# Convolution taps spread over the products of a stage, and a retention cut into 16 pieces between dense products

## The chip, the cores and the metric

One Trainium2 chip, of which the program uses one core. The metric is the device time of one execution in microseconds; the time of a kernel is the median of its runs. The engines of the core are named as in the profile: PE (TensorE matmuls) and PEld (its weight loads), DVE (VectorE), ACT (ScalarE), POOL (GpSimd), SP (SyncE, which issues the transfers).

## The reference

Two blocks follow one another, each with two layers, on a sequence of 1024 tokens of width 1024 in float32. A layer of the first block mixes three branches (a gated convolution of width 256, windowed attention, gated linear attention) and also carries a context of 256 tokens. A layer of the second block mixes spatial gating, a pooling over several scales and a retention, and has a feed-forward part behind it. The two parts that the change touches:

```python
def _conv_branch(p, conv_w, conv_b, ln_w, ln_b):        # first block
    u = p['a_val'] * jax.nn.sigmoid(p['a_glu'])
    u = lax.conv_general_dilated(u, conv_w[:, None, :], window_strides=(1,), padding=((15, 15),), ...,
                                 feature_group_count=256) + conv_b      # 31 taps, channel by channel
    u = (u - mean(u)) * lax.rsqrt(var(u) + NORM_EPS) * ln_w + ln_b
    return jax.nn.silu(u) * jax.nn.silu(p['a_gate'])

def retention(q, k, v, g, norm_g):                      # second block: 8 heads of 64, 8 chunks of 128
    ...
    scores = jnp.einsum('bnthd,bnshd->bnhts', qc, kc) * d_intra
    y_intra = jnp.einsum('bnhts,bnshe->bnthe', scores, vc)
    kv = jnp.einsum('bnshd,bnshe->nbhde', kc * k_dec[:, :, None], vc)
    _, s_prev = lax.scan(lambda state, kv_n: (state * chunk_dec + kv_n, state), zeros, kv)
    y_cross = jnp.einsum('bnthd,nbhde->bnthe', qc * q_dec[:, :, None], s_prev)
    y = group_norm(y_intra + y_cross)                   # mean and variance over each head's 64
    return jax.nn.silu(g) * (y * norm_g)
```

## The kernel before

**Dense products.** Every dense product is three matmuls of split operands (`mm3`, L211 to L213: hi × hi, hi × lo or lo × hi). ACT makes the high half of a weight (`whi`, L205), and its low half (`wlo`) is a subtraction on POOL (L190) or DVE (L192); in the projections of the first block four of six go to POOL (`LP_L1`). `gemm_fm` has the weights stationary: one product is 24 matmuls of 512 columns (or 256 for the context). `gemm_tm` has the tokens stationary: one token block is 24 matmuls of the weight's width (288 columns in `tm2`, 384 in `tm1`, 512 in `v` and `za`). After the evacuation of each product or token block `tick()` is called: it takes one mark off `self.ticks`, and when none is left it advances a generator, `self.side`, by one step. What a step emits lies behind that product in the program.

**Order on the engines.** A scheduler places the instructions; each engine runs its own queue in order. A high priority moves instructions ahead in it, and `in_order()` keeps PE's instructions of a block as they are written.

**The convolution (first block, both layers).** `conv_taps` (L469 on) makes 4 sums in layer 0, each of a first product and 30 taps on DVE (L482, L484): `ca20` and `ca21` for the context, 256 wide, and `ca00` and `ca01` for the sequence, 1024 wide. In layer 1 there are 60 taps, on 1024. Within a sum every tap reads the one before. All taps are emitted at once, before `qk`, with a high priority (offset -1500). `qk` makes the queries and keys, rotates them on DVE (`qt`, `qra`, `qrb`, `qa`, L821 to L827), splits them (`qlo`) and stores them over SP. Behind it `gla_proj` runs `tm2` (ten token blocks, with the copies `lr` and the gates `ggt`), the weights W12 and W11, and `tm1`. `conv_out` (the mean and variance over channels by matmuls with the constants `om` and `ones`, the normalisation and the gate) is the side generator of `gla_proj`, behind `CT` = 15 or 13 marks.

**The retention (second block, both layers).** `rotate` writes rotated queries and keys to memory. `gemm_tm` "v" makes the values of the eight blocks. Then `retention` emits all eight blocks in one go. Each has the scores of two groups of heads (L1234, 64 rows of the array each, first one half of the rows, then the other; the score times the decay is `ra`, L1236), the transposed keys (L1241, `kd` L1243), the score times the values (L1248), the state times the queries (L1256, one half of the rows after the other, `ry` L1257 and L1258), the new state (L1266, between halves of the columns; `rst` L1272 and L1273) and the norm of the result on DVE, POOL and ACT (`rmu`, `rv`, `rsq`, `rss`, with a power on POOL, L179). Keys and queries of each block come by transfer (L1227) in two buffers. The projection and the sums of the pooling (`pooling_in`, `pooling`) and the gating's projection `za` (`spatial_in`) follow.

## Time and profile before

| | |
|---|---|
| runs | 3634.89, 3642.01 and 3643.11 us, median 3642.01 |
| profiled execution | 3637.38 us, its span 3635.6 us |
| mean granted clock of PE | 0.975 |
| busy: PE, PEld | 3439.9 us (95%), 2757.1 us (76%) |
| busy: DVE, ACT, POOL | 2448.4 us (67%), 1209.4 us (33%), 848.1 us (23%) |

The profile is of one execution. The views below are: the page's account of the chain of work that ended last, by engine; stretches of time (start and end, length, then for PE, PEld, DVE, ACT and POOL the busy microseconds and in brackets the instructions, the clock granted to PE as a share of full speed, the share of the transfer engines and GB/s); the waits of an engine (the waiting line, the operation that released it, total, times, longest); pieces of the chain and instructions in time (start, duration, engine, line, operation, in square brackets the idle time ahead and what ended it); and groups of instructions (count, busy time, mean ns, idle time ahead). Names of tiles have their buffer numbers left out.

### The profile page before, as it was taken

Reading aid. Unit: us, or ns where it says so; the run is one execution under the profiler, and the core shown is the slowest. Engines: PE = TensorE matmul, PEld = TensorE weight load, DVE = VectorE, ACT = ScalarE, POOL = GpSimd, SP = SyncE. Lnnn points to the kernel's source line nnn. Section 1 sums busy time; section 2 is a strip of 40 time slices with the busy share of each in tenths; the row PEclk is TensorE's granted clock in tenths of the full one; section 3 lists DMA queues with packets and bytes.
Section 4 is the critical chain, followed back from the end, with each engine's and each line's share of the span. In section 5 each row is a group of like instructions: output and inputs, shape, how many; then the busy total and the mean of one; then the engine's idle time right before and its main releaser. Section 6 shows DMA issues by size and latency. Waiting matters only on the chain.

```text
span 3635.6 us, 47069 instructions
## 1 busy us (share of the span) xinstructions
PE 3439.9 (95%) x17414; PEld 2757.1 (76%) x17414; DVE 2448.4 (67%) x3786; ACT 1209.4 (33%) x2189; POOL 848.1 (23%) x700
## 2 busy tenths in 40 slices
PE   7959999998899999999999998999999989999898
PEld 4858766786776678887878776887887778877786
DVE  5963568569365867364599999446363589999545
ACT  4114236341251642213343334223112333334322
POOL 4331332112323222040133222001041132232100
PEclk9979999999899999999999999999999999999999
DMA  5221355533224234314422222434322522221532
GB/s 198 74 76 63 109 163 163 179 117 82 67 71 123 77 118 126 107 39 136 134 79 78 85 70 82 161 96 151 93 68 88 176 75 76 81 76 59 185 99 90
DMA packets 245973, 380.71 MB, mean 105 GB/s; under 512 B 29104, under 2 KB 103792, under 8 KB 245232
## 3 DMA queue, kind: packets, MB, share of 16 engines
q1 hardware_dynamic: 245744, 377.71, 33.4%
q8 instruction: 137, 2.24, 0.3%
q14 instruction: 92, 0.75, 0.1%
HBM read 280.35 MB, written 97.26 MB: 104 GB/s over the span
## 4 chain that ended last, share of the span: by engine, by line
PE 56%; DVE 15%; issue 5%; DMA 2%; ACT 2%; POOL 2%; SPq 0%; DVEq 0%; POOLq 0%; ACTq 0%
PE mm L213 10%; PE mm L211 10%; PE mm L212 10%; PE ax L211 3%; PE ax L213 3%; PE ax L212 3%; PE sc L211 3%; PE sc L213 3%; PE sc L212 3%; DVE wlo L192 2%; DVE cv L1427 2%; DVE ca L484 1%; DVE fth L331 1%; PE ax L1248 1%; PE sc L1234 1%
## 5 line engine op out<-in xcount | busy, mean ns | idle before, releaser
L211 PE MATMUL mm<-hi,whi 128*128 128x512 f32 (+1 forms) x1780 | 688.8, 387 | 22.5 <-ACT whi L205 12.4
L213 PE MATMUL mm<-hi,wlo 128*128 128x512 f32 (+1 forms) x1780 | 687.8, 386 | 5.1 <-DVE wlo L192 5.1
L212 PE MATMUL mm<-lo,whi 128*128 128x512 f32 (+1 forms) x1780 | 684.4, 385 | 1.2 <-DVE lo L1612 1.1
L205 ACT CAST whi<-wraw 128x512 fp32r<-128x512 f32 (+3 forms) x412 | 231.9, 583 | 583.9 <-PE mm L212 260.5
L192 DVE TENSOR_TENSOR wlo<-wraw,whi 128x512 fp32r<-128x512 f32 (+2 forms) x320 | 231.6, 738 | 279.0 <-ACT whi L205 277.6
L211 PEld LDWEIGHTS mm<-hi,whi 128*128 128x128 f32 x1780 | 336.6, 189 | 94.4 <-ACT whi L205 13.2
L213 PEld LDWEIGHTS mm<-hi,wlo 128*128 128x128 f32 x1780 | 336.0, 189 | 75.7 <-DVE wlo L192 8.2
L212 PEld LDWEIGHTS mm<-lo,whi 128*128 128x128 f32 x1780 | 336.4, 189 | 72.2 <-DVE lo L1612 3.1
L190 POOL TENSOR_TENSOR wlo<-wraw,whi 128x512 fp32r<-128x512 f32 (+3 forms) x92 | 138.3, 1510 | 796.4 <-ACT whi L205 768.6
L211 PE MATMUL sc<-hi,whi 128*128 128x512 f32 x732 | 288.4, 394 | 18.2 <-ACT whi L205 10.5
L213 PE MATMUL sc<-hi,wlo 128*128 128x512 f32 x732 | 288.5, 394 | 2.0 <-DVE wlo L192 1.9
L212 PE MATMUL sc<-lo,whi 128*128 128x512 f32 x732 | 287.6, 393 | 2.0 <-DVE lo L1612 1.9
L211 PE MATMUL mm<-whi,hi 128*128 128x512 f32 (+2 forms) x704 | 260.5, 370 | 20.9 <-ACT whi L205 15.7
L212 PE MATMUL mm<-wlo,hi 128*128 128x512 f32 (+2 forms) x704 | 256.3, 364 | 11.9 <-POOL wlo L190 10.8
L213 PE MATMUL mm<-whi,lo 128*128 128x512 f32 (+2 forms) x704 | 256.8, 365 | 0.0
L484 DVE SCALAR_TENSOR_TENSOR ca<-u,wh,ca 128x1024 f32<-128x1024 f32 (+1 forms) x180 | 184.6, 1079 | 0.6
L213 PE MATMUL ax<-hi,wlo 128*128 128x512 f32 x456 | 180.1, 395 | 2.4 <-DVE wlo L192 2.4
L211 PE MATMUL ax<-hi,whi 128*128 128x512 f32 x456 | 180.1, 395 | 1.8 <-DVE xn L1343 1.4
L212 PE MATMUL ax<-lo,whi 128*128 128x512 f32 x456 | 179.2, 393 | 0.0
L211 PEld LDWEIGHTS sc<-hi,whi 128*128 128x128 f32 x732 | 138.7, 189 | 49.3 <-ACT whi L205 11.2
L192 DVE TENSOR_TENSOR wlo<-wr,whi 128x512 fp32r<-128x512 f32 x200 | 175.3, 887 | 0.0
L211 PEld LDWEIGHTS mm<-whi,hi 128*128 128x128 f32 x704 | 134.5, 191 | 40.5 <-ACT whi L205 15.9
(376 smaller groups left out, 6737.5 us busy)
## 6 DMA issues: line engine op xcount, KB each, us to landing
wr<-in_w_up SPq DMA_DIRECT2D x80, 512.0 KB, 3.5
wraw<-in_w_fm SPq DMA_DIRECT2D x108, 256.0 KB, 3.1
wm<-in_w_mod SPq DMA_DIRECT2D x96, 256.0 KB, 3.7
wraw<-in_w_down SPq DMA_DIRECT2D x96, 256.0 KB, 2.7
hid_d<-fth SPq DMA_DIRECT2D x44, 512.0 KB, 2.6
wraw<-hid_d SPq DMA_DIRECT2D x88, 256.0 KB, 2.9
wraw<-in_w_out SPq DMA_DIRECT2D x80, 256.0 KB, 3.4
yl<-y_d SPq DMA_DIRECT2D x64, 256.0 KB, 3.1
```

The costliest lines, as they stand in the source:

```text
L190: nc.gpsimd.tensor_sub(out, x, f(hi))
L192: nc.vector.tensor_sub(out, x, f(hi))
L205: nc.scalar.copy(hi[:, c], r)
L211: nc.tensor.matmul(ps, sh, mh, start=start, stop=False)
L212: nc.tensor.matmul(ps, sh, ml, start=False, stop=False)
L213: nc.tensor.matmul(ps, sl, mh, start=False, stop=stop)
L331: nc.vector.scalar_tensor_tensor(out, tanh_tmp, 1.0, x, op0=ALU.add, op1=ALU.mult)
L484: nc.vector.scalar_tensor_tensor(a, u[:, j:j + n], wh[:, c, j:j + 1], a, op0=ALU.mult, op1=ALU.add)
L1234: nc.tensor.matmul(ps[:, m * 128:m * 128 + 128], k[r, m, :], q[r, m, :], start=True, stop=True)
L1248: nc.tensor.matmul(pi[:, hv], A[h % 2][:, h // 2, :], V[:, j, hv], start=True, stop=True)
L1427: nc.vector.scalar_tensor_tensor(t[:, o:], x[:, 0:S - o], wc(2 - o), t[:, o:], op0=ALU.mult, op1=ALU.add)
```

## The change

`conv_taps` becomes a generator. It yields after every tap of 1024 columns and after every fourth of 256, works one sum after the other (`ca20`, `ca21`, `ca00`, `ca01`), and has no priority. Each tap gets a dependency on the last `mm3` matmul emitted (`not_before`), which only the scheduler sees: it becomes no wait on the chip. The generator is advanced by the ticks of `qk` (one step a tick, two in the products of `ev_a`) and of `gla_proj` (two steps, and three from W12 on); `conv_out` is chained behind it.

`retention` becomes a generator of 16 pieces, two for a block. It is created ahead of "v" and advanced by its ticks (after two idle ones, `RT`), by those of `pooling_in` and by those of `za`; what is left runs behind `spatial_in`. Score matmuls and state matmuls now alternate between the two halves of the rows, in a fixed order. The keys and queries of the next block are loaded behind the first piece of a block; the values for the new state stand before the score times the values; `pooling` stands before `spatial_in`.

```diff
+    def not_before(self, ins):
+        self.tc.add_manual_dep(
+            ins.ins, self.mark.ins.name,
+            mybir.DependencyInfo(mybir.DependencyClass.NoSync, mybir.DependencyReason.SCHED_ONLY), reason="pace")
@@ mm3
-        nc.tensor.matmul(ps, sl, mh, start=False, stop=stop)
+        self.mark = nc.tensor.matmul(ps, sl, mh, start=False, stop=stop)
@@ tick
-                next(self.side, None)
+                for _ in range(self.pace):
+                    next(self.side, None)
@@ layer1
-                self.conv_taps(l, conv, cp)
+                taps = self.conv_taps(l, conv, cp)
+                self.ticks, self.side, self.pace = [], taps, 1
                 self.qk(l, W, both, al, rng)
...
-                    self.ticks = [None] * CT[l]
-                    self.side = self.conv_out(l, conv, cl)
+                    self.side, self.pace = chain(taps, self.conv_out(l, conv, cl)), 2
@@ conv_taps
-                with self.tc.high_priority(offset=-1500):
-                    nc.vector.tensor_scalar(a, u[:, 0:n], wh[:, c, 0:1], self.col("conv_b", 2 * l + c), op0=ALU.mult, op1=ALU.add)
-                    for j in range(1, 31):
-                        nc.vector.scalar_tensor_tensor(a, u[:, j:j + n], wh[:, c, j:j + 1], a, op0=ALU.mult, op1=ALU.add)
+                self.not_before(nc.vector.tensor_scalar(a, u[:, 0:n], ...))
+                for j in range(1, 31):
+                    self.not_before(nc.vector.scalar_tensor_tensor(a, u[:, j:j + n], wh[:, c, j:j + 1], a, ...))
+                    if j % (S // n) == 0:
+                        yield
@@ layer2
-            self.gemm_tm("v", I["w_tm_v"][l], 512, toks(), ev_v)
-                self.retention(l, V, rp, r1)
+                self.ticks = [None] * RT
+                self.side = self.retention(l, V, rp, r1)
+                self.gemm_tm("v", I["w_tm_v"][l], 512, toks(), ev_v)
                     xb = self.pooling_in(l, W, lat, mp)
+                    self.pooling(l, xb, mp)
                     z = self.spatial_in(l, toks, sp)
-                    self.pooling(l, xb, mp)
+                    run(self.side)
@@ retention
+            with self.in_order():
+                for m in range(4):
+                    for g, r in halves:
+                        nc.tensor.matmul(ps[g][:, m * 128:m * 128 + 128], k[r, m, :], q[r, m, :], start=True, stop=True)
...
+                nxt = load(j + 1)
+            yield
...
+                with self.in_order():
+                    for m in range(4):
+                        for g, r in halves:
+                            nc.tensor.matmul(pc[g][:, m, :], q[r, m, :], st[r, m, :], start=True, stop=True)
...
+            yield
```

On DVE in layer 0, where `qk` ends and `tm2` begins, the kernel before has the constants of `conv_out` (`lwh`, `om`) and the first copies of `tm2` behind the taps, of which only a few are left:

```order
L484 SCALAR_TENSOR_TENSOR ca_1000<-u_600,wh,ca_1000 128x1024
L484 SCALAR_TENSOR_TENSOR ca_968<-u_609,wh,ca_968 128x256
L484 SCALAR_TENSOR_TENSOR ca_1032<-u_603,wh,ca_1032 128x1024
L484 SCALAR_TENSOR_TENSOR ca_936<-u_606,wh,ca_936 128x256
L492 TENSOR_SCALAR lwh<-cols 128x1
L493 TENSOR_SCALAR lwh<-cols 128x1
L492 TENSOR_SCALAR lwh<-cols 128x1
L493 TENSOR_SCALAR lwh<-cols 128x1
L495 MEMSET om 128x128
L484 SCALAR_TENSOR_TENSOR ca_968<-u_609,wh,ca_968 128x256
L484 SCALAR_TENSOR_TENSOR ca_1000<-u_600,wh,ca_1000 128x1024
L550 COPY lr<-mm 128x32 x2
```

The changed kernel at the same place on DVE, where `ca_1473` is `ca00`, one of the two wide sums:

```order
L193 TENSOR_TENSOR qlo<-qa,qhi 128x256
L502 TENSOR_SCALAR lwh<-cols 128x1
L503 TENSOR_SCALAR lwh<-cols 128x1
L502 TENSOR_SCALAR lwh<-cols 128x1
L503 TENSOR_SCALAR lwh<-cols 128x1
L505 MEMSET om 128x128
L560 COPY lr<-mm 128x32
L491 SCALAR_TENSOR_TENSOR ca_1473<-u_600,wh,ca_1473 128x1024
L339 SCALAR_TENSOR_TENSOR ggt<-ggt,mm 128x256
L491 SCALAR_TENSOR_TENSOR ca_1473<-u_600,wh,ca_1473 128x1024
L560 COPY lr<-mm 128x32
```

What moved: `om` stands ahead of the first `lr`, and a tap stands behind each `lr` and each `ggt` of the ten token blocks.

Behind `tm2`, where the weights of `tm1` are split, DVE of the changed kernel has the rest of the taps; `ca_2138` is `ca01`, the last sum, and `rs` belongs to `conv_out`:

```order
L491 SCALAR_TENSOR_TENSOR ca_2138<-u_603,wh,ca_2138 128x1024
L193 TENSOR_TENSOR wlo<-wraw,whi 128x256
L491 SCALAR_TENSOR_TENSOR ca_2138<-u_603,wh,ca_2138 128x1024
L193 TENSOR_TENSOR wlo<-wraw,whi 128x512
L491 SCALAR_TENSOR_TENSOR ca_2138<-u_603,wh,ca_2138 128x1024 x28
L175 TENSOR_SCALAR rs<-ax 128x2
```

What moved: 28 taps of one sum stand here in one piece, which the kernel before has among the taps of all sums further ahead.

On PE in the retention of layer 0, one block of the kernel before, with four matmuls of another product between:

```order
L1234 MATMUL sc<-rq,rk 128x128 x8
L1241 MATMUL sc<-ident,rk 128x128 x4
L212 MATMUL mm<-lo,whi 128x512
L213 MATMUL mm<-hi,wlo 128x512
L211 MATMUL mm<-hi,whi 128x512
L212 MATMUL mm<-lo,whi 128x512
L1248 MATMUL ax<-rv,ra 128x64
L1256 MATMUL sc<-rst,rq 128x64 x4
L1248 MATMUL ax<-rv,ra 128x64 x7
L1256 MATMUL sc<-rst,rq 128x64 x4
L1266 MATMUL ax<-rv,kd 64x64 x8
```

One block of the changed kernel on PE, where "..." stands for the matmuls of one product:

```order
L220 MATMUL mm<-whi,lo 128x512
L1258 MATMUL sc<-rq,rk 128x128 x8
L1267 MATMUL sc<-ident,rk 128x128 x4
L218 MATMUL mm<-whi,hi 128x512
...
L220 MATMUL mm<-whi,lo 128x512
L1279 MATMUL sc<-rst,rq 128x64 x8
L1288 MATMUL ax<-rv,kd 64x64 x8
L1292 MATMUL ax<-rv,ra 128x64 x8
L218 MATMUL mm<-hi,whi 128x512
```

What moved: the block is two pieces, with the 24 matmuls of a whole product between them and behind them, and the eight state matmuls stand together.

## Rows read from the trace of the kernel before

**Rows 1.** The page's part 4: shares of the chain that ended last:

```profile
PE 56%; DVE 15%; issue 5%; DMA 2%; ACT 2%; POOL 2%; SPq 0%; DVEq 0%; POOLq 0%; ACTq 0%
```

**Rows 2.** Stretches of the first block's layer 0: busy us per engine, PEclk, DMA:

```profile
200.00:220.00 20.00, 0.00 (x0) 0.00 (x0) 20.00 (x26) 0.40 (x1) 4.09 (x1) 0.50 0.16 37
220.00:240.00 20.00, 9.58 (x57) 9.43 (x58) 14.87 (x27) 2.16 (x6) 9.71 (x6) 0.63 0.29 85
240.00:260.00 20.00, 20.00 (x149) 19.77 (x148) 5.86 (x14) 3.96 (x9) 6.08 (x8) 1.00 0.15 49
```

**Rows 3.** PE's waits, 90 to 240 us: total us, times, longest:

```profile
PE ax L499 <- DVE om L495: 35.9, 1, 35.9
PE mm L211 <- DVE qrb L825: 3.8, 2, 2.0
```

**Rows 4.** The same stretches in layer 1 of the first block:

```profile
900.00:920.00 20.00, 0.61 (x1) 0.29 (x1) 20.00 (x17) 1.01 (x3) 9.17 (x2) 0.51 0.33 79
920.00:940.00 20.00, 15.74 (x108) 15.74 (x109) 10.52 (x21) 1.54 (x4) 8.90 (x6) 0.81 0.19 60
```

**Rows 5.** PE's waits, 820 to 940 us:

```profile
PE mm L211 <- ACT whi L205: 15.7, 1, 15.7
PE mm L212 <- POOL wlo L190: 10.8, 1, 10.8
PE mm L211 <- DVE qrb L825: 3.9, 1, 3.9
```

**Rows 6.** Chain ahead of 924 us: start, us, what:

```profile
904.29 0.61 DVE qlo L192
...
910.45 2.09 DMA wraw<-in_w_tm
```

**Rows 7.** DVE in time, layer 0's first taps: start, us, operation:

```profile
94.92 10.53 DVE L484 SCALAR_TENSOR_TENSOR ca<-u,wh,ca 128x1024 f32<-128x1024 f32 x8
```

**Rows 8.** DVE in time, tokens of tm2:

```profile
239.79 0.19 DVE L550 COPY lr<-mm 128x32 f32<-128x32 f32 x1 [0.22 <-PE mm L213]
...
242.97 0.19 DVE L550 COPY lr<-mm 128x32 f32<-128x32 f32 x1 [0.59 <-PE mm L213]
243.66 0.42 DVE L331 SCALAR_TENSOR_TENSOR ggt<-ggt,mm 128x256 f32<-128x256 f32 x1 [0.50 <-ACT ggt L330]
```

**Rows 9.** DVE's groups, 262 to 340 us: count, busy us, mean ns:

```profile
L503 DVE TENSOR_TENSOR ca<-ca,ax 128x512 f32<-128x512 f32 (+1 forms) x6 | 3.3, 595 | 17.3 <-PE ax L499 17.3
```

**Rows 10.** POOL in time beside the taps of layer 0:

```profile
113.66 2.96 POOL L190 TENSOR_TENSOR wlo<-wraw,whi 128x512 fp32r<-128x512 f32 x2 [1.11 <-ACT whi L205]
...
141.00 10.99 POOL L190 TENSOR_TENSOR wlo<-wraw,whi 128x512 fp32r<-128x512 f32 x1 [10.77 <-ACT whi L205]
```

**Rows 11.** Stretches of the retention, second block's layer 0:

```profile
1560.00:1580.00 20.00, 20.00 (x144) 18.24 (x143) 12.00 (x24) 1.26 (x2) 7.61 (x10) 0.73 0.20 59
1580.00:1600.00 20.00, 19.83 (x144) 17.52 (x141) 12.65 (x24) 3.24 (x6) 7.77 (x8) 0.93 0.00 1
```

**Rows 12.** The chain through one block of the retention:

```profile
1543.45 1.64 PE sc L1234 x16
...
1545.68 0.23 PE mm L212
...
1546.78 1.03 PE sc L1256 x8
...
1549.52 1.03 PE sc L1256 x8
1550.55 0.62 PE ax L1266 x16
```

**Rows 13.** Groups of instructions, 1536 to 1592 us:

```profile
L179 POOL TENSOR_TENSOR rss<-rss,mhalf 128x8 f32<-128x8 f32 x6 | 9.9, 1648 | 17.6 <-DVE rss L174 17.6
L1236 DVE TENSOR_TENSOR ra<-sc,dm 128x512 f32<-128x512 f32 x14 | 9.3, 685 | 1.7 <-PE sc L1234 1.7
```

**Rows 14.** POOL's groups, 1595 to 1640 us:

```profile
L1154 POOL TENSOR_TENSOR s<-s 128x1024 f32<-128x1024 f32 x2 | 5.1, 2540 | 0.1
```

More of the change, by code (lines that the diff above doesn't have):

```diff
@@ L1 @@
 from contextlib import ExitStack, contextmanager
+from itertools import chain
 import numpy as np
@@ L95, in __init__ @@
         self.lo_n, self.lo_pool = 0, LP_REST
-        self.side = None
+        self.side, self.pace = None, 1
         self.meanwhile = None
@@ L1221, in retention, with load @@
         st = None
-        for j in range(8):
+        def load(j):
             tk = slice(j * 128, j * 128 + 128)
@@ L1228, in retention @@
                     out=t, in_=d[:, :, :, tk].rearrange("(m h) a f t -> (h a f) m t", h=2))
+            return q, k
+        halves = [(g, slice(64 * g, 64 * g + 64)) for g in range(2)]
+        nxt = load(0)
+        for j in range(8):
+            q, k = nxt
+            ps = [self.psC.tile([128, 512], F32, name="sc", tag="sc") for g in range(2)]
+            with self.in_order():
+                for m in range(4):
+                    for g, r in halves:
+                        nc.tensor.matmul(ps[g][:, m * 128:m * 128 + 128], k[r, m, :], q[r, m, :], start=True, stop=True)
             A = []
             for g in range(2):
-                ps = self.psC.tile([128, 512], F32, name="sc", tag="sc")
-                r = slice(64 * g, 64 * g + 64)
-                for m in range(4):
-                    nc.tensor.matmul(ps[:, m * 128:m * 128 + 128], k[r, m, :], q[r, m, :], start=True, stop=True)
                 a = rp.tile([128, 4, 128], F32, name="ra", bufs=3)
-                nc.vector.tensor_mul(a, ps.rearrange("p (h t) -> p h t", h=4), dm[:, g::2, :])
+                nc.vector.tensor_mul(a, ps[g].rearrange("p (h t) -> p h t", h=4), dm[:, g::2, :])
                 A.append(a)
@@ L1266, in retention @@
                     nc.tensor.matmul(pv[r, (h // 2) * 64:(h // 2) * 64 + 64], kd[:, h, :], V[:, j, hv], start=True, stop=True)
+            pi = self.psB.tile([128, 512], F32, name="ax", tag="ax")
+            for h in range(8):
+                hv = slice(h * 64, h * 64 + 64)
+                nc.tensor.matmul(pi[:, hv], A[h % 2][:, h // 2, :], V[:, j, hv], start=True, stop=True)
+            if j < 7:
                 ns = rp.tile([128, 4, 64], F32, name="rst")
```

36 lines of the change are left out of this document (19 added, 17 removed).

## The prediction

> **What bounds the kernel now.** I read the chain that ended last first. TensorE (PE) carries 56% of it and VectorE (DVE) 15% [rows 1]: a change off PE pays only in a stage where PE stands still. So I looked for PE's longest waits, stage by stage. They lie in the two stages that hold the convolution taps, the projections of the first block's layers 0 and 1.
>
> In layer 0, PE does nothing from 200 to 220 us while DVE is busy for all of the 20 us, and DVE has 14.87 of the next 20 [rows 2]. The list of PE's waits names one stop of 35.9 us, before the first matmul of `conv_out` (ax), until the memset of its constant `om`; two more stops, 3.8 us together, wait for a rotated query (qrb) [rows 3]. The memset is not slow. It stands in DVE's queue behind nearly all taps, and all of PE's `tm2` work stands behind the matmul that needs it. [...]
>
> In layer 1 the stops are 15.7 us for a weight (whi, from ScalarE, ACT), 10.8 us for its low half (wlo, from GpSimd, POOL) and 3.9 us for qrb [rows 5]: 30.4 us, with DVE again full [rows 4]. The chain shows that these are the taps too: a low half of the queries (qlo) leaves DVE only at 904.29, its stores fill SyncE's (SP's) queue, and the weight behind them is loaded from 910.45 on [rows 6].
>
> [...]
>
> **The taps, removed waits.** The taps are neither fewer nor shorter. They come later: with a few behind each product, qlo, qrb and the copies `lr` go through between them, and `om` is set ahead of the first `lr`. Layer 0 gains 35.9 + 3.8 = 39.7 us of waits, and 4.4 us of PE work (230.4 to 234.8) at full instead of half speed, 2.1: 41.8 us. Layer 1 gains 30.4 us, and 3.3 us of work after 924.3 (0.81 over 20 us is half speed until 927.6) give 1.7: 32.1 us.
>
> **The taps, what comes in their place.** DVE's room for the displaced taps is there: from 240 to 260 us it is busy for 5.86 of 20 [rows 2]. Four costs arise.
>
> (1) The pace in `tm2`. A token comes every 3.18 us (239.79 to 242.97), and its `lr` and `ggt` take DVE 0.19 and 0.42 [rows 8]. Two taps of 1024 now stand beside them; in one chain, where each tap needs the one before it, a tap takes 10.53/8 = 1.32 us [rows 7]. Together 3.25 us a token: DVE is as full as PE. A lag of 0.07 us a token costs 0.7 over ten tokens; if every `ggt`, which comes from ACT, holds the queue for some 0.8 us, it costs 9. I take 5 in layer 0 and 3 in layer 1, since the truth lies between and the next weight's half on DVE stands behind the tenth token.
>
> (2) The run at the end. By the order 28 taps of one chain (20 in layer 1) stand in one piece on DVE, 28 × 1.32 = 37 us. PE is not behind them directly: it has W12's end, W11 and `tm1` to do. But POOL must split `tm1`'s last weights during that run. Beside taps POOL took 1.5 us for a split at 113.66 (two in 2.96), and 10.99 at 141.00 [rows 10]. Where the split goes through as at 113.66 the cost is 0; where it waits for the run to end, PE has W11 (24 matmuls of 0.23 us [rows 12] for each half of the tokens, 11 us) and some 4 us of the first token to do, so 37 − 15 = 22 us are lost in layer 0, and 20 × 1.32 − 15 = 11 in layer 1. I take 2 and 1: of 34 splits by POOL in the two tap stages three took over 6 us.
>
> [...]
>
> (3) The tail. `conv_out` now starts its wide parts late, two or three parts in `tm1`. Each is a chain of some eight DVE instructions of 0.6 us [rows 9] with PE, POOL and ACT between them, and its matmuls stand less than a token apart on PE. If PE waits half such a chain at each of three parts it is 8 us; if the scheduler's spacing holds, nothing. I take 4 and 3.
>
> (4) The order hint itself adds no semaphore, so no engine waits for it; it costs nothing.
>
> Layer 0: 41.8 − 5 − 2 − 4 = 31 us. Layer 1: 32.1 − 3 − 1 − 3 = 25 us.
>
> **The retention.** A block in the middle begins at 1543.45 and the next 7.7 us later. The score matmuls (L1234) take 1.64 us, the two state groups (L1256) 1.03 each, the value groups (L1266) 0.62 for 16 instructions [rows 12]. L1234 and L1256 finish one half of the rows before the other begins; L1266 alternates between two halves of the columns and needs 0.04 us an instruction, the others 0.10 to 0.13. After the change scores and states alternate between the row halves. If that does nothing, they stay at 1.64 and 2.06; if it does what L1266 shows, both fall to 0.62. I take 1.1 and 1.03, two halves side by side for the state and somewhat less for the scores. That saves 0.54 in each of 8 blocks and 1.03 in 7, 11.5 us a layer, 23 in both. The clock: with 5.5 us of dense work between pieces I expect no half speed, 13.6 us of which cost 6.8 (layer 0 alone shows it).
>
> The new waits: each piece stands in PE's fixed order between two products, and a piece whose operands are late now stops the products behind it. A block is two pieces and two products, about 5.2 + 11 = 16 us. Its work on DVE, POOL and ACT, read from 1560 to 1580 where 2.6 blocks pass, is (12.00 + 7.61 + 1.26)/2.6 = 8.0 us even end to end [rows 11]. So the pieces are covered, with some 8 us to spare, except where the pooling's additions stand ahead on POOL, 2.5 us each [rows 14], six a layer. 0 if the spare time takes them, 8 if four in a row meet one block; I take 3 a layer. Loads of keys and queries are issued a block ahead, with 11 us of products to land in; what SP has queued behind those that wait for a buffer (W1, za's weights) has the same cover. If it is gone, each load costs its landing time, 2 to 3 us like the 2.09 of [rows 6]. Retention: 23 + 6.8 − 6 = 24 us.
>
> **Sum.** 31 + 25 + 24 = 80 us. The profiled execution took 3637.4, so 3557.4; it was 4.6 us under the median of the runs, so 3562.
>
> **Rivals.** (a) *POOL is starved.* The last splits of `tm1` wait for the tap runs: 22 − 2 and 11 − 1 come back, 30 us, 3592. For it: 10.99 us at 141.00, in an unbroken run. Against it: a single chain leaves a gap of some 0.05 us between taps, and most splits got through. (b) *The row halves don't overlap.* The pieces cost PE what they did before, and only the clock is won: 3562 + 23 = 3585. For it: no row shows alternating row halves. Against it: L1266. (c) *The other side: the retention's round trip is longer than its cover.* Every block runs DVE, POOL, ACT and DVE in turn, with a power on POOL of 1.65 us and two score products of 0.69 on DVE at its ends [rows 13], and DVE is shared with the evacuations. Each microsecond by which the trip exceeds 16 us stops PE for one in each of 16 blocks. The gain of 80 us is gone from 5 us over on, at 21 us a block; at 23 it is 3562 + 16 × 7 = 3674. Against it: 8.0 us of work in a block. (d) *The hint doesn't hold on the chip.* It orders only the scheduler's own clock; if DVE runs behind it, the tap that should lie behind one product lies ahead of the next one's evacuation, and DVE bounds `tm2` and the queries as before: half of the two layers' 56 us come back, 3590.
>
> **How the numbers follow.** Chances: forecast 0.60, (a) 0.15, (b) 0.09, (d) 0.07, (c) 0.09, of which 0.06 end slower and 0.03 near no change. A change of 0.3%, 11 us, is about what a measurement of this kernel can tell. Faster: 0.60 + 0.15 + 0.09 + 0.07 = 0.91; same 0.03; slower 0.06. The low end: all terms at their good bounds, that is no wait in pace, run and tail (18), none in the retention (6), and row halves better than taken (12): 3562 − 36 = 3526. The high end must hold (a), (b) and (d), each with the tail and the pace at their bad bounds, some 20 more: 3612.
>
> **What would show it.** Right: no PE wait over 10 us between 90 and 340 us and in layer 1's stage; `om` done before the first `lr`; in the retention 16 score instructions in about 1.1 us and no stretch below clock 1.00. Wrong: a wait of PE for POOL's wlo at the start of `tm1` (a); 1.6 us for the scores and 2.06 for the state (b); PE waiting for ra, kd or rst ahead of L1292 or L1279 in most blocks (c); PE waiting for `lr`'s buffer or qrb, with DVE full, in layer 0 (d).

## The result, and the profile after

The changed kernel took 3607.47 us (median of 4 runs, 3600.90 to 3612.17), the kernel before 3642.56 us beside it: a ratio of 0.9903, with a 95% interval of 0.9879 to 0.9928. It is faster, by some 35 us. The forecast was 3562, a gain of 80. The direction and the range (3526 to 3612) held; the size did not, and 45 us are to be explained.

The profiled execution took 3606.73 us, its span is 3604.9, and the mean granted clock is 0.977. Its chain of waits by engine answers to [rows 1]:

```profile
PE 68%; DVE 15%; issue 5%; DMA 3%; POOL 3%; ACT 2%; SPq 1%; DVEq 0%; POOLq 0%; ACTq 0%
```

**Layer 0 of the first block.** PE's longest waits from 80 to 360 us (waiting line, what it waited for, total us, times, longest) answer to [rows 3]:

```profile
PE ax L509 <- DVE om L505: 13.5, 1, 13.5
PE ax L296 <- POOL rs L180: 4.6, 3, 3.2
```

The stop for `om` is 13.5 us, not gone. DVE in time (start, us, operation) shows that it is no longer the taps that hold it:

```profile
193.72 0.43 DVE L193 TENSOR_TENSOR qlo<-qa,qhi 128x256 fp32r<-128x256 f32 x1 [3.06 <-DMA qs_d<-qlo]
202.92 0.15 DVE L502 TENSOR_SCALAR lwh<-cols 128x1 f32<-128x1 f32 x1 [8.77 <-DMA qsc_d<-qhi]
...
203.23 0.17 DVE L505 MEMSET om<- 128x128 f32 x1
211.13 0.19 DVE L560 COPY lr<-mm 128x32 f32<-128x32 f32 x1 [7.74 <-PE mm L220]
```

DVE is idle from 194 us. It waits for a store of a query half (`qsc_d<-qhi`) to land, since the constants `lwh` and `om` take over memory of those halves. SP's own queue shows why the store is late:

```profile
181.19 1.71 SPq L769 DMA_DIRECT2D qs_d<-qhi  x4
...
201.75 1.76 SPq L769 DMA_DIRECT2D qsc_d<-qlo  x4
203.55 1.37 SPq L205 DMA_DIRECT2D wraw<-in_w_tm  x3
204.97 0.43 SPq L557 DMA_DIRECT2D gnw<-in_gla_norm  x1
```

From 181.19 to 203.51 SP issues the stores of the last six query tiles without a pause, 48 of 32 rows each, one every 0.47 us. The last three weight loads of `tm2` and the load of `gnw` (the norm weights of the gated attention) stand behind them. The kernel before has the same order on SP: there these loads went out at 221.76 us, while PE waited for `om`, which was set at 230.11 (SP's line and DVE's line of the kernel before):

```profile
221.76 1.37 SPq L204 DMA_DIRECT2D wraw<-in_w_tm  x3
```

```profile
230.11 0.17 DVE L495 MEMSET om<- 128x128 f32 x1
```

So `om` and the weights of `tm2` were both late before, and only the later one showed. What follows the stop begins at half speed, which ends between 210 and 220 us; the stretches (columns as in [rows 2]) are:

```profile
200.00:210.00 10.00, 4.71 (x14) 3.50 (x15) 0.48 (x5) 1.01 (x3) 1.86 (x3) 0.50 0.40 104
210.00:220.00 10.00, 10.00 (x61) 9.88 (x61) 8.87 (x12) 1.16 (x3) 4.09 (x3) 0.78 0.23 78
220.00:240.00 20.00, 18.06 (x133) 17.54 (x133) 20.00 (x25) 3.98 (x9) 12.54 (x8) 1.00 0.12 40
```

**Layer 1 of the first block.** The longest wait from 760 to 930 us answers to [rows 5]; here SP issues the last weights of `tm2` at 889.15 us, again right behind the stores (SP's line below the wait):

```profile
PE mm L218 <- ACT whi L206: 10.4, 1, 10.4
```

```profile
889.15 1.40 SPq L205 DMA_DIRECT2D wraw<-in_w_tm  x3
```

**The tail.** DVE runs the last taps in one piece, with `conv_out`'s `rs` behind it, and POOL gets its two splits of `tm1` through during it (DVE's line, then `rs`, then POOL's line):

```profile
258.61 38.20 DVE L491 SCALAR_TENSOR_TENSOR ca<-u,wh,ca 128x1024 f32<-128x1024 f32 x28
296.73 0.15 DVE L175 TENSOR_SCALAR rs<-ax 128x2 f32<-128x2 f32 x1
```

```profile
268.55 3.40 POOL L191 TENSOR_TENSOR wlo<-wraw,whi 128x512 fp32r<-128x512 f32 x2 [10.41 <-ACT whi L206]
```

PE's clock falls in this stretch; in the kernel before it was 1.00 in each 10 us from 290 to 340:

```profile
290.00:300.00 10.00, 6.83 (x36) 6.52 (x35) 7.46 (x9) 0.97 (x4) 1.73 (x3) 0.82 0.05 14
300.00:310.00 10.00, 10.00 (x47) 8.86 (x46) 2.88 (x6) 2.19 (x5) 0.06 (x1) 0.84 0.10 33
```

**The retention.** A block in the chain answers to [rows 12]: the row halves do run side by side, scores in 1.09 us (1.64 before) and both state groups in 1.04 (2.06).

```profile
1605.19 1.09 PE sc L1258 x16
...
1612.08 1.04 PE sc L1279 x16
1613.12 1.93 PE ax L1292 x16
```

But PE has a new stop in each layer, and half speed behind it. The waits of layer 0 (1440 to 1640 us) and of layer 1 (2560 to 2740), and the stretches, which answer to [rows 11]:

```profile
PE sc L1279 <- DVE ra L1262: 1.8, 2, 1.6
...
PE sc L1279 <- DVE ra L1262: 2.9, 1, 2.9
```

```profile
1560.00:1580.00 20.00, 18.37 (x113) 14.88 (x111) 12.29 (x18) 4.01 (x8) 10.32 (x8) 0.91 0.14 42
1580.00:1600.00 20.00, 20.00 (x123) 16.55 (x123) 7.01 (x13) 2.84 (x7) 2.88 (x3) 0.83 0.00 1
2680.00:2700.00 20.00, 17.06 (x99) 14.05 (x99) 8.97 (x16) 2.06 (x6) 5.07 (x5) 0.74 0.09 27
```

The granted clock is 0.50 or 1.00 in the profiles of both kernels (in this one 0.50 from 1578 to 1586 us and 1.00 from 1588 to 1600), so 0.91, 0.83 and 0.74 are 3.6, 6.8 and 10.4 us at half speed. PE's order points to the cause, which experiment 5 tests: `za` computes its first two tokens as a pair and ticks twice behind it, so both pieces of block 5 stand within six matmuls, and the second meets `ra` before DVE has it.

**Where the time went, stage by stage.** An instruction that both traces have starts at some time after each span's start, and the difference shows the gain so far: DVE's first `la<-sc,cols` of layer 0 after the convolution starts at 350.15 us before and at 342.10 after, 8.05 earlier. How that difference changes over a stage is the stage's gain (medians over the shared instructions of DVE, ACT and POOL). The last two columns are two of the experiments below.

| stage (us of the trace before) | forecast | after | two_queues | queues_and_tick |
|---|---|---|---|---|
| first block, layer 0: 80 to 350 | 31 | 7.9 | 24.3 | 23.0 |
| first block, layer 1: 770 to 1400 | 25 | 8.8 | 21.5 | 25.2 |
| retention, layer 0: 1440 to 1670 | 15.3 | 10.6 | 11.7 | 16.3 |
| retention, layer 1: 2540 to 2760 | 8.5 | 1.5 | 2.8 | 9.4 |
| all else | 0 | 1.9 | -8.4 | -12.6 |

"All else" is work that no edit touches. It holds, for one, a stretch at half speed near 465 us that shows in some executions and not in others (460 to 480 us: clock 0.66 and 0.82 before, 1.00 in the changed kernel), and, in two_queues and queues_and_tick, some 3 us that are lost within the first 80 us. A stage can hold such a stretch too: from 1100 to 1120 us two_queues is at 0.50, which costs its layer 1 some 5 us that the edit has no part in.

### The profile page after: what moved, and what is told of

The parts are those of the page before. It is cut to its first block, busy times and chain, and to the rows that moved or that the text cites. A ratio compares the mean times of both kernels' runs of the same rounds, so it can differ in the third digit from the quotient of the medians.

```text
span 3604.9 us, 47054 instructions
## 1 busy us (share of the span) xinstructions
PE 3435.6 (95%) x17414; PEld 2741.0 (76%) x17414; DVE 2451.5 (68%) x3786; ACT 1209.9 (34%) x2189; POOL 842.7 (23%) x700
## 4 chain that ended last, share of the span: by engine, by line
PE 68%; DVE 15%; issue 5%; DMA 3%; POOL 3%; ACT 2%; SPq 1%; DVEq 0%; POOLq 0%; ACTq 0%
PE mm L218 12%; PE mm L219 12%; PE mm L220 12%; PE ax L218 4%; PE ax L220 3%; PE ax L219 3%; PE sc L218 3%; PE sc L220 3%; PE sc L219 3%; DVE ca L491 3%; DVE wlo L193 2%; PE mm L938 2%; PE mm L952 2%; PE ax L713 1%; DVE cv L1460 1%
## 5 line engine op out<-in xcount | busy, mean ns | idle before, releaser
L218 PE MATMUL sc<-hi,whi 128*128 128x512 f32 x732 | 289.7, 396 | 18.7 <-ACT whi L206 10.6
L191 POOL TENSOR_TENSOR wlo<-wraw,whi 128x512 fp32r<-128x512 f32 (+3 forms) x92 | 119.6, 1304 | 704.6 <-ACT whi L206 639.1
L491 DVE SCALAR_TENSOR_TENSOR ca<-u,wh,ca 128x1024 f32<-128x1024 f32 (+1 forms) x180 | 204.7, 1141 | 3.7
L1429 ACT CAST whi<-wr 128x512 fp32r<-128x512 f32 x240 | 142.5, 614 | 72.1 <-POOL wr L1443 40.6
```

Source lines behind the costliest of these rows:

```text
L191: nc.gpsimd.tensor_sub(out, x, f(hi))
L218: nc.tensor.matmul(ps, sh, mh, start=start, stop=False)
L491: self.not_before(nc.vector.scalar_tensor_tensor(a, u[:, j:j + n], wh[:, c, j:j + 1], a, op0=ALU.mult, op1=ALU.add))
L1429: nc.scalar.copy(hi[:, c], x)
```

## Experiments

Each was run beside the kernel before on the same chip; ratios are to it, with 95% intervals.

**1. The parts alone.** The convolution's change without the retention's, and the reverse.

> Changed kernel with the retention, the pooling's place and the v product as they were before: the taps alone. From the two traces, by the same instructions, layer 0 and layer 1 of the first block gained 8.1 and 8.4 us, a half-speed stretch at 460 us that is missing by chance 4.4, and the retention 10.4 and 2.5 us. So the taps alone should give 3642 less 16 to 21 us, 3621 to 3626, and the retention's windows should look as in the kernel before. If the retention's pieces cost something elsewhere (code, transfers), the taps alone give more than that.

Measured 0.9947 (0.9916 to 0.9978): 19 us (8 to 31) of the 56 forecast.

> The kernel before with the change of the retention alone; the taps as before. The whole change is 0.9903 of before, the convolution alone 0.9947. Theory I (the two parts are independent): 0.9948 to 0.9965, that is 13 to 19 us less than before, about two thirds of the 24 us forecast for the retention. Rival J (the retention is worth its forecast of 24 us and loses part of it only beside the moved taps): 0.9925 to 0.994. Either way the two half speed stretches behind za's pair stand in its profile, with PE waits for ra of 1.5 to 3 us, one in each layer.

Measured 0.9937 (0.9919 to 0.9956): 23 us of before's 3651, rival J's range. The waits for `ra` are there as expected (1.6 and 2.9 us), the half speed behind them in layer 1 only. So the retention is worth its forecast of 24 by the medians, although the changed kernel's profiled execution shows 12 in the two layers. Why these differ is to be seen in conv_only's trace, whose retention is that of the kernel before:

```profile
1520.00:1540.00 20.00, 20.00 (x138) 18.35 (x137) 10.80 (x21) 3.16 (x6) 6.95 (x8) 0.68 0.43 129
1540.00:1560.00 20.00, 20.00 (x113) 18.45 (x113) 8.27 (x16) 0.63 (x1) 4.38 (x7) 0.50 0.13 39
1560.00:1580.00 20.00, 20.00 (x129) 18.03 (x128) 9.38 (x19) 1.26 (x2) 6.19 (x6) 0.67 0.14 41
1580.00:1600.00 20.00, 19.82 (x150) 17.75 (x149) 13.77 (x26) 1.85 (x3) 7.70 (x9) 0.87 0.05 15
```

That is 12.8 + 20 + 13.2 + 5.2 = 51 us at half speed where [rows 11] have 13.6, with PE full all the time. So the unbroken retention's clock was not the same in these two executions, and the profiled execution of before was the better one. That this difference also makes the spread of the runs is likely and not shown: the ten of conv_only spread over 36 us, with a mean granted clock of 0.981 in the fastest and 0.971 in the slowest, the four of the changed kernel over 11. The missing 37 us (25 to 48) lie in the convolution.

**2. The store queue ahead of `tm2`: fewer stores, more buffers, earlier constants.** one_store is the changed kernel with

```diff
-        for h in range(4):
-            self.nc.sync.dma_start(out=dst[h], in_=x[32 * h:32 * h + 32])
+        self.nc.sync.dma_start(out=dst, in_=x)
```

> Changed kernel, but each half of a query tile goes to memory in one transfer instead of four of 32 rows, so that the 48 issues on SP behind the last products of qk (181.2 to 203.5 us in layer 0, 0.47 us each) become 12. Theory S (SP's queue of stores is what the tap spreading ran into): the weights of tm2 are issued some 14 us earlier after the last store, PE's waits of 13.5 us (om) in layer 0 and 10.4 us (whi) in layer 1 fall under 4 us each, the half-speed stretch behind each goes with them (2 to 3 us each); the time falls by 15 to 22 us from the changed kernel's 3607, to 3585 to 3592. Rival D (DVE's order, not SP, holds om and the weights): the waits stay within 3 us of 13.5 and 10.4 and the time within 5 us. Rival T (the store itself, not its issue, is slow): the issues get shorter but the constants of conv_out still wait for the stores to land, and half of the wait stays.

Measured 0.9876 (0.9858 to 0.9895). In layer 1 the 10.4 us wait went, in layer 0 `om`'s, but waits of 5.7 (for `lr`) and 3.9 (for `ggt`) came in layer 0 and one of 6.5 (for `ggt`) in layer 1. Twelve issues in place of 48 are not faster. From 200 to 210 us the merged stores leave at this rate (last three columns: clock, share of the transfer engines, GB/s), and the last one is issued at 211.32, where the changed kernel is through with the separate ones at 203.51:

```profile
200.00:210.00 10.00, 0.79 (x2) 0.20 (x2) 5.22 (x8) 1.37 (x4) 0.00 (x0) 0.72 0.26 102
```

The changed kernel's separate stores have a share of 0.50 and 120 GB/s from 190 to 200 us. Both shares count all transfers of their 10 us; why the merged store has the lower one was not shown.

The two buffers do not set this rate: with four, in the next run, it is 104 GB/s at a share of 0.28 in the same stretch (101 at 0.26 in more_ggt, 4 below, which has four too).

store_buffers gives one_store four buffers for `qhi` and `qlo` in place of two.

> The kernel of one_store with four buffers instead of two for the halves qhi and qlo. In one_store the queue of issues is gone but in layer 0 ACT's qhi, POOL's and DVE's qlo waited for earlier stores to land (34, 37 and 14 us in sum), the last store left at 211 us and PE waited 5.7 us for lr and 3.9 for ggt behind those halves on DVE. Theory B (two buffers of stores are the next bound): the last stores leave before 200 us, PE's waits between 185 and 225 us fall from some 18 us to under 8, layer 0 gains 6 to 12 us on one_store, layer 1 no more than 3; 3584 to 3594 against one_store's 3601. Rival V (DVE is full in qk's last products, so the halves come late for that): the waits move to qrb and the time stays within 4 us of one_store.

Measured 0.984 (0.9788 to 0.9891), but a wait of 13.1 us behind DVE's `ggt` came: POOL's product with `gnw` waited for that load, issued behind the stores at 207.36.

early_consts makes `lwh`, `om` and `gnw` ahead of `qk`, in memory of their own.

> Changed kernel, but the constants of conv_out (lwh, om) and the norm weights of the gated attention (gnw) are made ahead of qk in memory of their own; in the changed kernel they lie in memory that the halves of the queries use until their last store has landed, and gnw's load stands behind the stores on SP. The four stores a half stay. Theory M (the shared memory is what holds om): the 13.5 us in layer 0 go, and 8 us or more of them are gained. Theory S (SP's queue of 48 issues holds the last weights of tm2 as well): the wait of 13.5 us for om turns into one of 10 to 14 us for whi or wlo of tm2, layer 1 keeps its 10.4 us, and the time stays within 5 us of the changed kernel's 3607.

Measured 0.9871 (0.9813 to 0.9928). This is theory S: the wait for `om` became one of 15.0 us for `whi`, which is made from the weights behind the stores, now issued at 205.96 us:

```profile
PE mm L218 <- ACT whi L206: 15.0, 1, 15.0
```

So `om` alone did not hold the stop: with `om` early the loads behind the stores hold PE as long. Layer 1 keeps its wait (10.7 us), and the ratio's interval holds the 0.9903 of the changed kernel.

consts_stores has all three edits.

> The kernel of early_consts with one store a half and four buffers for the halves. Theory S and M together (either alone keeps PE waiting, so only both help): PE's waits between 185 and 225 us in layer 0 fall under 6 us in sum, from 17.5 in the changed kernel and 16.8 in store_buffers (13.1 of them for ggt, behind gnw, whose load was issued at 207 and landed at 215 us); layer 0 gains 12 to 20 us on the changed kernel, layer 1 10 to 14; 3573 to 3585. If DVE is the bound there anyway, the waits move to qrb, lr or ggt behind taps on DVE and the gain of layer 0 stays under 6 us.

Measured 0.9827 (0.9779 to 0.9875), with 9.4 us left in layer 0: ACT's third `ggt` waited for a store of `gg_d`, behind the query stores once more.

all_four puts store_buffers, one_tick (5) and wide_first (4, below) together. It was expected at 3553 to 3571 us if the effects add, over 3580 if DVE bounds the stage of the taps. Measured 0.9824 (0.9779 to 0.987), 3585.98 us: they did not add, and what held PE was `ggt` again, 10.4 us in layer 0 and 10.3 in layer 1.

**3. The same queue, halved.** two_queues leaves everything as in the changed kernel and issues the stores of the high halves from ACT (`store_heads` takes the queue as an argument; the line that calls it is shown).

```diff
-    self.store_heads(d[g, :, i, ab, :, o:o + n], f(t[:, :n]))
+    self.store_heads(d[g, :, i, ab, :, o:o + n], f(t[:, :n]), nc.sync if i else nc.scalar)
```

> The changed kernel, and the high halves of the first block's query tiles are stored by ACT's queue (right behind the cast that makes them), the low halves by SP as before; still four stores of 32 rows each. Traces so far: SP issues these stores every 0.47 us, so they leave at 135 to 145 GB/s; merged into one store a half they leave at only about 100 GB/s, though fewer have to be issued. Theory D (it is the rate at which one queue drains the stores that holds tm2's weights, constants and gg_d in layer 0): the last query store is issued some 8 to 10 us earlier than 203.5, the PE wait of 13.5 us in layer 0 (om) and of 10.4 us in layer 1 (whi) fall to 6 or less each; 12 to 20 us less than the changed kernel, ratio to before 0.985 to 0.987. Rival E (the transfer engines are the limit, not the queue): both queues slow each other down, the last store lands within 3 us of before, 0.989 to 0.991.

Measured 0.9814 (0.9791 to 0.9837), more than any theory gave: with two queues 32 us more are gained (0.9903 to 0.9814). The longest waits are now

```profile
PE mm L218 <- DVE ggt L339: 6.6, 1, 6.6
PE mm L218 <- DVE qrb L835: 3.0, 1, 3.0
```

in layer 0, and at most 2.4 us in layer 1. But the mechanism is not the rate that I expected to show. SP's timeline:

```profile
168.97 0.42 SPq L205 DMA_DIRECT2D wraw<-in_w_tm  x1
170.00 1.69 SPq L768 DMA_DIRECT2D qsc_d<-qlo  x4
178.33 1.46 SPq L205 DMA_DIRECT2D wraw<-in_w_tm  x2
...
199.73 1.82 SPq L768 DMA_DIRECT2D qsc_d<-qlo  x4
```

The last group of stores starts only 2.0 us earlier than 201.75. What moved is the order: with half as many stores in its way, the scheduler placed `tm2`'s last weight loads between them, 25 us earlier than 203.55, and PE works on `tm2`'s tokens while the last stores go out (columns as in [rows 2]; the changed kernel, then two_queues):

```profile
190.00:200.00 10.00, 0.05 (x1) 0.00 (x0) 1.09 (x2) 0.81 (x2) 0.73 (x1) 0.70 0.50 120
```

```profile
190.00:200.00 10.00, 10.00 (x63) 10.00 (x63) 3.79 (x6) 2.10 (x5) 4.36 (x4) 0.79 0.60 162
```

The scheduler moved a second thing: the first matmul that needs `om` stands ahead of most of `tm2` in the changed kernel and behind all of it in two_queues, where `om` itself is set later, at 208.52 us (the changed kernel, then two_queues):

```profile
203.54 1.19 PE L509 MATMUL ax<-ca,om 128*128 128x256 f32 x2 [13.49 <-DVE om L505]
```

```profile
285.14 0.59 PE L509 MATMUL ax<-ca,om 128*128 128x256 f32 x2
```

So two_queues takes both late operands out of `tm2`'s way in layer 0, and does not tell them apart there. early_consts does: with `om` early, the loads alone held PE for 15.0 us. In layer 1 the wait was for the weights from the start. Loads behind stores on one queue were the cause, with `om` held by the same stores; the time of the last store, which moved by 2.0 us, was not. The rate with two queues is 150 GB/s from 180 to 190 us against 112 for one, at shares of 0.53 and 0.47; what limits it no run here tests. One issue is small (0.47 us against 1.7 from issue to landing), but 24 fewer are 11 us of SP's queue, and the loads behind them went out 25 us earlier.

**4. Is it only the order of one queue, or are there others behind it?** best is the sum of consts_stores with one_tick (5), slow_out and wide_first (4, below).

> All that the runs so far speak for: early constants, one store a half with four buffers, one tick for the pair of za, wide sums first with 18 taps (12 in layer 1) ahead of qk, conv_out at one step a tick. If the terms add (layer 0: 12 to 20 from stores and constants, 6 from the wide sums; layer 1: 10 and 0 to 4; retention 13), 3607 less 41 to 53, 3554 to 3566; with DVE as the bound of the tap stages 3575 or more.

Measured 0.979 (0.9745 to 0.9835), 3578.09 us, with a wait of 12.0 us for `ggt` left in layer 0. Three variants of it ask what holds that: six buffers for `ggt`, and the second queue with separate and with merged stores.

> The best version so far (constants ahead of qk, one store for each half of a query tile, four buffers for them, za's pair ticking once, wide sums first, conv_out one step a tick), and in tm2 six buffers in place of two for ggt, the tile that is stored to gg_d. That version still has one PE wait of 12.0 us in layer 0, behind DVE's third ggt; ACT waits there for a store of gg_d, which stands behind the query stores in SP's queue. Theory T (the buffer and SP's queue behind it hold PE): no PE wait over 4 us from 180 to 260 us in layer 0, and 12 to 16 us less than the version without (ratio to before 0.9747 to 0.9765 where that had 0.979). Rival U (DVE or a load is next): the wait moves to lr, gnw or wlo, with at most 4 us gained (0.978 or more).

Measured 0.9826 (0.9795 to 0.9857), rival U: the wait grew to 19.7 us. ACT now waits for the last query store itself, whose memory the new buffers take over:

```profile
215.43 0.66 ACT L343 ACTIVATE ggt<-mm 128x256 f32<-128x256 f32 x2 [19.26 <-DMA qsc_d<-qlo]
```

> The version named best (constants ahead of qk, four buffers for the halves, za's pair ticking once, wide sums first, conv_out one step a tick), but with the query stores of the first block as four of 32 rows each again, high halves by ACT's queue, low halves by SP's. Theory D: the PE wait of 12.0 us behind ggt in layer 0 falls to 4 or less, and the half speed stretch behind it goes; 10 to 16 us less than best, ratio to before 0.975 to 0.9765. Rival E: the wait stays over 8 us, 0.978 to 0.981.

> As best_two_queues, but each half stored in one transfer of 128 rows, as in best. If the 100 GB/s of such stores is a limit of each queue, two queues give 200 and the result is that of best_two_queues (0.975 to 0.9765); if the few transfer engines that share such a store are the limit (a share of 0.2 of the 16 in best's trace), the ggt wait stays over 8 us (0.978 to 0.981).

Measured 0.9807 (0.9781 to 0.9833) and 0.9809 (0.9782 to 0.9836): no gain on best. With separate stores the `ggt` wait fell to 0.9 us as theory D has it, but waits for `wlo` (4.1 and 3.2) and `qra` (4.1) took its place, so the time is rival E's though its wait is not. With merged stores 7.7 us for `ggt` stay, just under the 8 that were expected if the few transfer engines are the limit; the two queues have 120 GB/s at a share of 0.33 from 200 to 210 us, not 200. One cure is enough here; several do not add.

The tail and the taps ahead had runs of their own. early_taps does 12 tap steps ahead of `qk`; slow_out advances `conv_out` one step a tick; wide_first has slow_out, the wide sums first and 18 taps ahead of `qk`.

> Changed kernel, but 12 steps of the taps (12 times 4 taps of 256 columns in layer 0, 12 taps of 1024 in layer 1) are emitted before qk, without a product between them. Theory R (the 28 and 20 taps in one piece behind tm2 make conv_out late, and its parts then stand on PE without work between): the runs shrink to under 15 taps, PE's waits for rs of conv_out (4.6 us in layer 0, 2.4 in layer 1) and the half-speed stretches from 290 to 340 us go, the gain at the end of tm1 grows by 6 to 12 us in layer 0 and by 3 to 9 in layer 1; the time falls by 10 to 20 us to 3587 to 3597. Rival D2 (the loss behind tm2 comes from DVE being full in tm2, not from the run): less than 4 us. The waits of 13.5 and 10.4 us ahead of tm2 should stay as they are in both.

Measured 0.9927 (0.9909 to 0.9945): theory R fell. The last run shrank from 28 taps to 16, the tail's wait stayed (`rs` 4.1 us), and DVE held the queries back:

```profile
PE ax L511 <- DVE om L507: 13.4, 1, 13.4
PE mm L218 <- DVE qt L787: 8.0, 1, 8.0
```

> Changed kernel, but conv_out is advanced by one step a tick in tm1, where it had three (so that the mean, the reciprocal root and its spreading over the rows of one part stood on PE without a product between). Theory O (the three steps in one tick make the waits for rs): the waits for rs (4.6 us in layer 0, 2.4 in layer 1) fall under 1.5 us and the half-speed stretches between 290 and 340 us go; 6 to 10 us less in layer 0 and 2 to 6 in layer 1 at the end of tm1. Against it: steps that no longer fit in tm1's ticks run behind it with nothing between, and the loss moves there; then the time stays within 4 us of 3607.

Measured 0.9911 (0.9878 to 0.9944): the wait for `rs` fell to 1.6 us and the half speed went, but the steps left over ran behind `tm1`. Nothing was gained.

> The kernel of slow_out, and the sums of 1024 columns come first, with 18 of their taps ahead of qk and free of the order hint, so that DVE works from 95 to 120 us, where the changed kernel leaves it idle (12.9 of 40 us busy from 80 to 120). By the order the long run behind tm2 is gone (the taps left there are of 256 columns). Theory R2 (run and steps together make the tail): the loss behind tm2 (12 us in layer 0, 9 in layer 1) falls under 4 us in each; the 13.5 and 10.4 us ahead of tm2 stay; 3586 to 3596. Rival K (what DVE does early it owes to the rotation of the keys, as in early_taps, where PE waited 8.0 us for qt): a wait for qt or qrb of 4 us or more and no gain.

Measured 0.9888 (0.9843 to 0.9933), inconclusive against 0.9903: 6.6 us earlier in layer 0, nothing gained in layer 1 (1.0 us lost over its stage), where queries now wait for `qt` (4.5 us).

**5. The two pieces at `za`'s pair.** one_tick lets the pair tick once; pool_behind ties the pooling's sums behind `za` instead, which takes POOL and DVE away from the block.

```diff
-                self.tick()
+                if name != "za" or key != 0:
+                    self.tick()
```

> Changed kernel, but the first two token blocks of za, which are computed as a pair, advance the retention by one piece and not by two. Theory P (the pair puts both pieces of block 5 within six matmuls on PE, so that the second waits for DVE with no product to cover it): the waits for ra (1.6 us in layer 0, 2.9 us in layer 1) and the half-speed stretches behind them (10 us at half speed in each layer, worth 5 us each) go; the time falls by 8 to 15 us to 3592 to 3599. Rival Q (the pooling's sums on POOL and DVE stand ahead of block 5's chain, whatever the spacing): the waits stay at 1 us or more at the piece that follows the sums, and the time falls by less than 5 us.

Measured 0.9873 (0.9855 to 0.9891), 11 us better than the changed kernel by the ratios, whose intervals overlap a little; the trace is clearer, and speaks for theory P. In layer 0 the wait for `ra` is 0.2 us, in layer 1 none is listed, and the retention is 6.0 and 7.0 us shorter in the two layers.

```profile
PE sc L1280 <- DVE ra L1263: 0.2, 1, 0.2
```

> Changed kernel, but the first two sums of the pooling are tied behind the last product of za in the scheduler's order, so that on POOL they stand behind all blocks of the retention. Rival Q (see the run with one tick): the waits for ra and the half-speed stretches of block 5 go, the time falls by 8 to 15 us unless the sums are late for the output stage. Theory P: the wait at the pair shrinks but does not go, since scores to ra, kd and back still need 2 to 3 us with six matmuls (1.4 us) between; the clock may still fall, and the time falls by 0 to 8 us.

Measured 0.9937 (0.9911 to 0.9963): the wait went too, but the sums then come late for the second block's output, and both layers are longer (6.7 and 5.2 us). In layer 1 PE also waits 8.0 us for the low halves of weights. So the wait for `ra` needs both, the pieces together and the sums ahead; of the two edits tried, only the first took one away at no cost.

**6. Both causes and nothing else.** queues_and_tick is two_queues with one_tick.

> The changed kernel with the two edits that each answer one cause found so far, and nothing else: the high halves of the first block's query tiles stored by ACT's queue, and the first pair of za's tokens ticking once. Alone the first took the changed kernel from 0.9903 of before to 0.9814, the second to 0.9873. If the two causes are separate, the gains add: 0.9903 - 0.0089 - 0.0030 = 0.978, that is 0.9765 to 0.980, with no PE wait for ra and no stretch under clock 0.95 from 1520 to 1640 us. If one edit only moves the other's loss (the retention's clock depends on where the first block ends, say), 0.981 or more.

Measured 0.9801 (0.9774 to 0.9829), 3573.29 us, the lowest median of all versions; 0.0013 behind two_queues, where 0.003 was expected, which the intervals do not tell apart. The traces do, by stage: the last column of the table above has 23.0, 25.2, 16.3 and 9.4 us against forecasts of 31, 25, 15.3 and 8.5. Layer 0 of the retention is at full speed:

```profile
1540.00:1560.00 20.00, 20.00 (x117) 16.00 (x118) 11.58 (x17) 5.11 (x11) 10.42 (x7) 1.00 0.11 37
1560.00:1580.00 20.00, 20.00 (x154) 16.71 (x152) 8.48 (x17) 2.87 (x8) 3.51 (x4) 1.00 0.06 15
1580.00:1600.00 20.00, 20.00 (x117) 16.20 (x116) 9.10 (x16) 5.13 (x11) 4.32 (x6) 1.00 0.05 15
```

## Why the prediction was right or wrong

**The range held by luck.** Its high end was made for rivals (a), (b) and (d), and none of them happened; 3607 came mostly from stops that the sum had as gone. Of the four signs of being right two held (`om` ahead of the first `lr`, scores in about 1.1 us) and two failed (waits of 13.5 and 10.4 us, a clock down to 0.74 in the retention). The 12 us for better row halves in the low end are 13.5 by the rows that they come from.

**Wrong: "Layer 0 gains 35.9 + 3.8 = 39.7 us of waits", and layer 1 30.4.** This is the step that failed. It took a wait as gone with its cause. Before, `om` was set at 230.1 us and SP issued the weights of the same stage at 221.76: two things were late, and the list of waits names the later one. The sum asked what is late next for each new cost, but not for the removed wait. For layer 0 the answer stood in SP's queue, for layer 1 even in [rows 6], where the weight behind the stores is loaded at 910.45; I read that row as "the taps hold the stores" and took it that the stores would then cost nothing, though 48 of them take SP 22 us, longer than what is left of `qk` to cover them. The prediction gave what SP has queued a price only in the retention. In layer 0 the stop fell by 35.9 - 13.5 = 22.4 us, in layer 1 from 30.4 to 10.4 and smaller ones. In layer 0, of the missing 23 us, 16 are missing ahead of the tail: the gain stands at 18.7 us at 280 us, where 41.8 - 5 - 2 = 34.8 were forecast. two_queues, whose edit changes only who issues the stores (the order that the scheduler then chose changed with it), is 11 us ahead of the changed kernel just behind the stop in layer 0 (31 against 20 us gained by 240 us) and 12 in layer 1 (30 against 18 by 930 us): so much of the missing 23 and 16 us is this step. The 2.1 us that the sum gives layer 0 for work at full instead of half speed no run shows: before, PE works for 3.6 us from 230 to 234 us at a clock of 0.50, and behind the shorter stop of the changed kernel for 8.7 us from 200 to 214 us, at 0.50 too.

**Wrong in size: "(3) The tail. ... I take 4 and 3."** It is the rest of the loss in layer 0: the gain stood at 18.7 us at 280 us of the trace before and at 8.1 at 350, 11 given back where 4 were allowed; in layer 1 some 5 (24.8 at 960 us, 19.3 at 1050) where 3 were. About half of it in layer 0 is waits (4.6 us for `rs`), and about half the granted clock behind them (0.82, 0.84 and, from 320 to 330 us, 0.83 are 10.2 us at half speed, 5 lost), which no term had. `conv_out`'s three steps come in one tick, so the scheduler's spacing that the step named does not exist there. No run cured the tail alone at a profit. But in two_queues and queues_and_tick, whose edits do not touch it, the same stretch of layer 0 gives back 5.6 and 7.1 us, with 1.8 us of waits for `rs`: a third to a half of this loss came with the order that the store queue led to, and why is open.

**Wrong: "A block is two pieces and two products, about 5.2 + 11 = 16 us".** True for 7 of 8 blocks. At `za`'s first pair two ticks follow each other and a block has no product between its pieces. The new-wait term (3 us a layer) was about the wait's size (1.6 and 2.9 us) and left out the clock: 3.6 + 6.8 us at half speed cost 5 in layer 0, 10.4 cost 5 in layer 1. one_tick and the last column of the table show that this was the whole of it: 16.3 and 9.4 us where 15.3 and 8.5 were forecast.

**Right: row halves.** 1.1 and 1.03 were taken, 1.09 and 1.04 measured; rival (b) fell. **Right: the retention as a whole**, 23 us by ret_only, though part of it is a clock that varies from run to run and was read from one execution only. The 6.8 us for the clock are worked out from [rows 11], where 0.73 and 0.93 are 10.8 and 2.8 us at half speed; no run shows them as a fixed gain: conv_only's unbroken retention has 51 us at half speed, the changed kernel 10.4 in each layer, and queues_and_tick none from 1520 to 1600 us.

**Right in the main: the pace and the run.** From 220 to 240 us PE is busy for 18.06 of 20, and tokens come every 3.2 us; from 240 to 280 us the gain falls by 1.4 us, where the pace was allowed 5 (in layer 1, from 930 to 960 us, by 4.5 where it was allowed 3). POOL's two splits took 3.40 us inside the run of 28 taps, so rival (a) did not happen. In the kernel before, [rows 10] have 1.5 and 10.99 us for the same split beside taps of several sums, so what decides it stays open. In the run each tap starts 0.036 us after the end of the one before, where the prediction had some 0.05.

**Right: the hint and the displaced taps.** The last low half of the queries leaves DVE at 193.72 us (215.88 before), `om` stands ahead of `lr`, and no PE wait in layer 0 names DVE's taps; rivals (c) and (d) fell.

**Open.** What keeps layer 0 at 23 to 24 of 31 us once the queue is mended: the waits left (6.6 for `ggt`, 3.0 for `qrb`) would account for it, but no run took them away without a new one. A run that moves the loads ahead of the stores and nothing else was not made. A store of one issue that has the separate stores' share of the transfer engines (0.50 against 0.26) was not tried.

## What to carry to other kernels

When a long wait is to be removed, look at every other operand that the waiting stage needs and read when each of them became ready; what the removal brings is the distance to the second latest, which here was in the queue that issues the transfers. Count how long a queue needs for the stores that stand ahead of the next stage's loads (here 22 us for 48), and try another queue for them if it is more than the work that covers them (two_queues: 0.9814 against 0.9903). When work is cut in pieces that ride on the ticks of other loops, look for the place where two ticks come together.

## What the runs showed of the hardware

The merged store is the slower one: transfers of 128 rows move at 102 GB/s at a share of 0.26 of the transfer engines (one_store, 200 to 210 us), those of 32 rows at 120 at a share of 0.50 (the changed kernel, 190 to 200 us), though they take four issues of 0.47 us. A short stop of PE can cost more than itself: behind stops of 1.6 and 2.9 us in the retention 10.4 us each ran at half speed in the changed kernel, worth some 5 us each, but in ret_only the same 1.6 us stop was followed by full speed, so it is not certain in every execution. The unbroken retention had 13.6 us at half speed in the profiled execution of before and 51 in that of conv_only, with PE busy all through in both; one profiled execution is a thin base for a term on the clock.
